# The order of TensorE's products in a planned kernel: products of one kind kept together, a larger reserve of buffers

## The chip, the cores and the metric

One core of one Trainium2 chip runs the kernel. The metric is the device time of one launch in microseconds (us); before the change it is 470.25 us, the median of 3 runs (469.52 to 470.39). The engines are TensorE (PE in the profile: matrix products; PEld: loading their weights), VectorE (DVE), ScalarE (ACT), GpSimd (POOL) and SyncE (SP), which issues DMA transfers.

## The reference

One layer of a hybrid decoder for a prompt of 1024 new tokens and 8 sequences of 8 sample tokens, 1088 tokens of 1024 features. All is float32. Cut to what matters:

```python
h = rms_norm(x, norm_g)
a, gl, zc, q, k, v, zg, lr = split(h @ w_in)            # 1024 x 3088
# group 1: a causal convolution
u  = a * sigmoid(gl)
cv = depthwise_causal_conv(u, conv_w, conv_b)           # 31 taps, 512 channels
cv = silu(group_layer_norm(cv, cn_g, cn_b))
cv = (cv @ w_pw + b_pw) * silu(zc)
# group 2: gated linear attention, 4 heads, keys 64, values 128
g  = log_sigmoid(lr @ w_alpha + b_alpha) / 16           # lr has rank 16
# per chunk of 64 tokens, B = cumsum(g):
o  = (q * exp(B)) @ S + mask((q * exp(B)) @ (k * exp(-B)).T) @ v
S  = S * exp(B_last) + (k * exp(B_last - B)).T @ v
o  = rms_norm_per_head(o) * gla_g * silu(zg)
y  = rms_norm(x + concat(cv, o) @ w_out, final_g)
```

Besides y the kernel writes the last 30 rows of u and the states S, for the prompt and for each sample.

## The kernel before

Features or channels lie on the 128 partitions, tokens along the free axis. The tokens are cut into chunks of 384, 384 and 320 (line 24), the last 64 of which are the sample tokens. The large products are made in three passes of the type f32r, each factor split into a high and a low part (hh and hl of the normed input, h_ and l_ of a weight); in the profile p_a, p_gl, p_q, p_k, p_zc and p_zg are such projections by chunk, and pv0_0 to pv0_8 and pv1_0 to pv1_8 the value projection by tiles of 128 tokens for the two pairs of heads (v_tile, line 645). Small products, transposes and the attention are plain f32: lrtp (a transpose), pk (transposed keys), px (keys times values), pa (scores), po (outputs, from the state S and from the masked scores at), pos, pas and pSs (samples).

The tile pv0_n also carries the 16 gate features. VectorE splits them into the buffers lrst0 and lrst1 in turn; TensorE transposes such a buffer (lrtp, lines 690 and 691), ScalarE copies it to lrT, and from three of these the gates of a chunk are made (gates, line 705: a product pg, then exp, ln, a cumulative sum B as a scan on VectorE, and the factors ge and g). Only then can q, k and the attention of that chunk follow (gla_states, line 765; gla_out, line 797). The heads are normed by o_norm (line 918): ScalarE squares o into osq, the square is split into on_h and on_l, TensorE sums each over the partitions (on_2p for the third chunk), and VectorE scales o.

The depthwise convolution runs on VectorE: for each of four tiles of channels 31 instructions over 1024 tokens (SCALAR_TENSOR_TENSOR cv<-u,par,cv; the first is a TENSOR_SCALAR), called taps here. For the samples ScalarE writes the 31 scaled rows into pr, and VectorE adds them up in two TENSOR_REDUCEs (conv_start, line 551).

The order of the instructions isn't written out by hand. Each instruction is recorded as an Op with a cost in ns (add, line 142; the costs stand at the helpers, lines 320 to 398) and a priority, which is its number in the program's order; taps get 1048576 more (conv_tick) and so fill whatever else leaves free. The planner (schedule, lines 183 to 290) then plays the program on a model of the engines: whenever an engine is free it takes from the instructions whose inputs are ready the one of the lowest priority whose buffers can be had. The buffers are slots of a few tags ("unit": 11 of 128x384); can_alloc (line 212) leaves free slots for tiles that come earlier in the program, at most as many as the tag's reserve says. In the order of the planned starts the instructions are issued (issue, line 292), each engine runs its own in that order, and the semaphores between them are set by the data. The plan's times thus set the order on every engine, and nothing else.

## Time and profile before

| | |
|---|---|
| device time, median of 3 runs | 470.25 us (469.52 to 470.39) |
| the profiled execution | 470.04 us |
| its span | 467.9 us |
| mean granted clock of TensorE | 0.995 of full |
| TensorE busy | 458.9 us (98%) |
| VectorE busy | 401.1 us (86%) |
| ScalarE busy | 304.4 us (65%) |
| TensorE busy from 36 to 450 us | 414.00 of 414.00 us |

The span runs from the first instruction to the last; the execution's time has some 2 us more around it. A busy share counts the time in which at least one instruction of the engine is under way. Instructions of one engine overlap at their ends: a tap lasts 1.28 us and the next one starts 1.20 us after it, and a product's record is longer than the distance to the next. What an instruction costs its engine is therefore the distance between starts, not its length. A granted clock of 1.00 is the upper of TensorE's two levels, 2.4 GHz.

### The profile page before, as it was taken

What the parts mean: (1) busy time and instruction counts of PE and PEld (TensorE: products, weight loads), DVE (VectorE), ACT (ScalarE), POOL (GpSimd) and SP (SyncE); (2) the same over time, 40 slices, a digit from 0 to 9 for tenths busy, and PEclk for the clock granted to TensorE, in tenths of its full rate; (3) what the DMA queues carried; (4) which work ended last, traced back from release to release, by engine and by line L of the source; (5) the groups of instructions that cost most, each with busy time, mean ns of one, the idle gap of its engine ahead of it and who ended that gap; (6) DMA issues with size and microseconds to landing.
All of it is one profiled execution on the core that took longest, in us unless ns stands there. A gap on an engine that the chain in (4) does not pass through costs nothing.

```text
span 467.9 us, 7864 instructions
## 1 busy us (share of the span) xinstructions
PE 458.9 (98%) x2867; PEld 431.2 (92%) x2867; DVE 401.1 (86%) x634; ACT 304.4 (65%) x780; POOL 19.3 (4%) x39
## 2 busy tenths in 40 slices
PE   8999999999999999999999999999999999999994
PEld 7899999999999999999999999999999988888783
DVE  4999998999999989999888999995548848988674
ACT  6978649926670545685634696544899548878636
POOL 1000000000000000000000000000000023130000
PEclk9999999999999999999999999999999999999998
DMA  8910283313012110022021011102235392386754
GB/s 253 352 57 1 93 205 57 54 51 69 1 59 78 36 56 6 35 73 77 20 71 39 14 47 45 46 22 73 88 78 181 87 228 48 68 182 154 242 174 179
DMA packets 33238, 43.28 MB, mean 92 GB/s; under 512 B 11696, under 2 KB 16560, under 8 KB 33200
## 3 DMA queue, kind: packets, MB, share of 16 engines
q1 hardware_dynamic: 30896, 38.59, 26.5%
q0 software_dynamic: 2304, 4.20, 5.5%
q8 instruction: 22, 0.36, 0.3%
q14 instruction: 16, 0.13, 0.1%
HBM read 36.58 MB, written 6.19 MB: 91 GB/s over the span
## 4 chain that ended last, share of the span: by engine, by line
PE 88%; DMA 4%; DVE 3%; ACT 3%; issue 1%; SPq 1%; DVEq 0%
PE pv L389 11%; PE p_zc L389 10%; PE p_zg L389 10%; PE p_gl L389 8%; PE p_a L389 8%; PE ya L389 7%; PE p_k L389 5%; PE p_q L389 5%; PE pw L389 5%; PE yc L389 5%; PE po L389 2%; PE pys L389 2%; DMA xr<-in_x 1%; DVE xr L343 1%; DMA s_gl<-in_w_in 1%; DMA s_a<-in_w_in 1%
## 5 line engine op out<-in xcount | busy, mean ns | idle before, releaser
L339 DVE SCALAR_TENSOR_TENSOR cv<-u,par,cv 128x1024 f32<-128x1024 f32 x120 | 150.8, 1278 | 0.2
L389 PE MATMUL pv<-h_v,hh 128*128 128x272 f32 (+1 forms) x128 | 37.4, 292 | 0.0
L389 PE MATMUL pv<-h_v,hl 128*128 128x272 f32 (+1 forms) x128 | 37.1, 290 | 0.0
L389 PE MATMUL pv<-l_v,hh 128*128 128x272 f32 (+1 forms) x128 | 36.8, 288 | 0.0
L333 ACT ACTIVATE pr<-us,par 128x64 f32<-128x64 f32 x124 | 32.3, 343 | 2.4 <-DMA us<-in_cc 2.4
L389 PE MATMUL p_gl<-hh,h_gl 128*128 128x384 f32 (+1 forms) x96 | 32.5, 339 | 0.8 <-ACT hh L333 0.8
L389 PE MATMUL p_zc<-hh,h_zc 128*128 128x384 f32 (+1 forms) x96 | 32.0, 333 | 0.0
L389 PE MATMUL p_gl<-hl,h_gl 128*128 128x384 f32 (+1 forms) x96 | 31.7, 330 | 0.2 <-DVE hl L343 0.2
L389 PE MATMUL p_a<-hh,l_a 128*128 128x384 f32 (+1 forms) x96 | 31.8, 331 | 0.0
L389 PE MATMUL p_a<-hh,h_a 128*128 128x384 f32 (+1 forms) x96 | 31.5, 328 | 0.1
L389 PE MATMUL p_zc<-hh,l_zc 128*128 128x384 f32 (+1 forms) x96 | 31.5, 329 | 0.0
L389 PE MATMUL p_zc<-hl,h_zc 128*128 128x384 f32 (+1 forms) x96 | 31.5, 328 | 0.0
L389 PE MATMUL p_gl<-hh,l_gl 128*128 128x384 f32 (+1 forms) x96 | 31.5, 328 | 0.0
L389 PE MATMUL p_zg<-hh,l_zg 128*128 128x384 f32 (+1 forms) x96 | 31.5, 328 | 0.0
L389 PE MATMUL p_zg<-hl,h_zg 128*128 128x384 f32 (+1 forms) x96 | 31.4, 327 | 0.0
L389 PE MATMUL p_zg<-hh,h_zg 128*128 128x384 f32 (+1 forms) x96 | 31.4, 327 | 0.0
L389 PE MATMUL p_a<-hl,h_a 128*128 128x384 f32 (+1 forms) x96 | 31.4, 327 | 0.0
L389 PEld LDWEIGHTS pv<-h_v,hh 128*128 128x128 f32 x128 | 24.1, 188 | 0.6 <-issue 0.2
L389 PEld LDWEIGHTS pv<-h_v,hl 128*128 128x128 f32 x128 | 24.1, 188 | 0.3 <-issue 0.3
L389 PEld LDWEIGHTS pv<-l_v,hh 128*128 128x128 f32 x128 | 24.1, 189 | 0.2
L389 PEld LDWEIGHTS p_gl<-hh,h_gl 128*128 128x128 f32 x96 | 18.1, 189 | 1.7 <-ACT hh L333 1.2
L389 PEld LDWEIGHTS p_gl<-hl,h_gl 128*128 128x128 f32 x96 | 18.2, 189 | 0.9 <-DVE hl L343 0.5
(337 smaller groups left out, 1306.8 us busy)
## 6 DMA issues: line engine op xcount, KB each, us to landing
xr<-in_x SPq DMA_DIRECT2D x16, 256.0 KB, 4.4
out_y<-xr SPq DMA_DIRECT2D x16, 256.0 KB, 2.3
x<-in_xT SPq DMA_DIRECT2D x16, 192.0 KB, 4.5
T<-in_w_out POOLq DMA_DIRECT2D x12, 256.0 KB, 5.1
s_gl<-in_w_in SPq DMA_DIRECT2D x8, 256.0 KB, 4.9
s_a<-in_w_in SPq DMA_DIRECT2D x8, 256.0 KB, 4.1
s_zc<-in_w_in SPq DMA_DIRECT2D x8, 256.0 KB, 2.6
s_zg<-in_w_in SPq DMA_DIRECT2D x8, 256.0 KB, 2.7
```

The lines of the kernel that those rows point to most:

```text
L333: return S.activation(R(out), R(in_), func, **kw)
L339: return prog.add("DVE", lambda: V.scalar_tensor_tensor(R(out), R(a), R(s), R(b), op0, op1), [out], [a, s, b], out.n / 0.96 + 67 + 62 * is ...
L343: return prog.add("DVE", lambda: V.tensor_tensor(R(out), R(a), R(b), op), [out], [a, b], out.n / 0.96 + 67)
L389: o = prog.add("PE", lambda: T.matmul(R(ps), R(lhsT), R(rhs), start=start, stop=stop, skip_group_check=True), [ps], [lhsT, rhs], c / 2 if ...
```

## The change

The planner's model of TensorE and its choice are changed in four places. (1) Each TensorE Op gets a kind, true for f32r products and false for plain f32 ones and transposes. When TensorE is free, the planner also looks for the ready Op of lowest priority among those of the kind that ran last; if its number is less than that of the best Op plus 60 (STICK), it is taken instead. For such a choice can_alloc is asked strictly, so that all earlier tiles' slots are left free. (2) A change of kind is charged 90 ns in the plan. (3) An f32r product is charged n/2.4 + 14 ns in place of n/2.4 + 2.5 for n columns. (4) The reserve of the tag "unit" is 8 in place of 6.

```diff
--- before.py
+++ after.py
@@ -47,6 +47,7 @@
 STATES_AT = 1
 CN_LAST = 2
 ADD_LAG = 5000
+STICK = 60
 SQ_SUM = (2, 4, 8)
 MARGIN = 20
 NWARM = 10
@@ -126,7 +127,7 @@
 
 class Op:
     __slots__ = ("eng", "fn", "cost", "lag", "table", "prio", "seq", "deps", "users", "wait", "ready", "tiles",
-                 "allocs", "start", "end", "bytes", "name")
+                 "allocs", "start", "end", "bytes", "name", "kind")
 
 
 class Program:
@@ -139,9 +140,10 @@
         self.last_pe = None
         self.chain = None
 
-    def add(self, eng, fn, outs, ins, cost, table=None, nbytes=0, lag=0):
+    def add(self, eng, fn, outs, ins, cost, table=None, nbytes=0, lag=0, kind=None):
         o = Op()
         o.eng, o.fn, o.cost, o.table, o.bytes, o.lag = eng, fn, cost, table, nbytes, lag
+        o.kind = kind
         o.seq = len(self.ops)
         o.prio = o.seq + (LOW if self.low else 0)
         if eng == "PE" and self.step:
@@ -208,15 +210,18 @@
         holder = {}
         dma = [0.0, 0.0]
         done = []
-
-        def can_alloc(o, t):
+        kind = [None]
+
+        def can_alloc(o, t, strict=False):
             need = {}
             for tl in o.tiles:
                 if tl.tag in free_at and tl.slot is None:
                     need.setdefault(tl.tag, []).append(tl.first)
             for tag, firsts in need.items():
                 have = sum(1 for f in free_at[tag] if f <= t)
-                before = min(bisect_left(pend[tag], min(firsts)), self.reserve.get(tag, 1 << 30))
+                before = bisect_left(pend[tag], min(firsts))
+                if not strict:
+                    before = min(before, self.reserve.get(tag, 1 << 30))
                 if have < len(firsts) + before:
                     return False
             return True
@@ -230,18 +235,24 @@
             t, e = heapq.heappop(events)
             if t < t_free[e]:
                 continue
-            best = None
+            best = same = None
             nxt = None
             for o in avail[e]:
                 if o.ready <= t:
                     if (best is None or o.prio < best.prio) and can_alloc(o, t):
                         best = o
+                    if (e == "PE" and o.kind == kind[0] and (same is None or o.prio < same.prio)
+                            and can_alloc(o, t, True)):
+                        same = o
                 elif nxt is None or o.ready < nxt:
                     nxt = o.ready
             if best is None:
                 if nxt is not None:
                     heapq.heappush(events, (nxt, e))
                 continue
+
+            if same is not None and same.prio < best.prio + STICK:
+                best = same
             o = best
             avail[e].remove(o)
             o.start = t
@@ -249,6 +260,9 @@
             if o.table is not None and table[0] != o.table:
                 table[0] = o.table
                 cost += 1300
+            if e == "PE" and o.kind != kind[0]:
+                kind[0] = o.kind
+                cost += 90
             if e == "SP":
                 t_free[e] = t + 60
                 dma[0] = max(dma[0], t) + 450
@@ -313,7 +327,7 @@
     ctx = ExitStack()
     V, S, G, T = nc.vector, nc.scalar, nc.gpsimd, nc.tensor
     prog = Program({"big": NBIG, "unit": NUNIT, "wst": NST, "wl": NW, "wh": NW, "ps": 8, "kT": 2, "S": 6, "ss": 9},
-                   {"ps": 3, "unit": 6, "big": 2})
+                   {"ps": 3, "unit": 8, "big": 2})
 
     TABLES = {AF.Exp: "natural_log_exp_and_others", AF.Ln: "natural_log_exp_and_others",
               AF.Sigmoid: "sigmoid_and_others", AF.Silu: "silu_and_others"}
@@ -385,9 +399,9 @@
     def mm(ps, lhsT, rhs, start, stop, after=(), pair=False):
         n, m = rhs.n, lhsT.n
         lag = 150 if m <= 64 and not R_DT(rhs) else 0
-        c = max(n / 2.4 + 2.5, m / 1.2) if R_DT(rhs) else max(n / 1.2 + 2.5, m / 1.2) + max(n / 1.2 if m > 64 else 53, m / 1.2)
+        c = max(n / 2.4 + 14, m / 1.2) if R_DT(rhs) else max(n / 1.2 + 2.5, m / 1.2) + max(n / 1.2 if m > 64 else 53, m / 1.2)
         o = prog.add("PE", lambda: T.matmul(R(ps), R(lhsT), R(rhs), start=start, stop=stop, skip_group_check=True),
-                     [ps], [lhsT, rhs], c / 2 if pair else c, lag=lag)
+                     [ps], [lhsT, rhs], c / 2 if pair else c, lag=lag, kind=R_DT(rhs))
         o.deps.update(a for a in after if a is not None)
         return o
 
@@ -395,7 +409,7 @@
         return v.tile.dt == F32R
 
     def transpose(out, in_, idn):
-        return prog.add("PE", lambda: T.transpose(R(out), R(in_), R(idn)), [out], [in_, idn], 109)
+        return prog.add("PE", lambda: T.transpose(R(out), R(in_), R(idn)), [out], [in_, idn], 109, kind=False)
 
     with ctx:
         fixed = ctx.enter_context(tc.tile_pool(name="fixed", bufs=1))
```

All engines have the same instructions as before, in another order. Lines of the kernel after are 14 higher where they lie behind line 212 or so (L389 becomes L403).

VectorE before the change, where the gates of tiles 5 to 7 are prepared (lrst1 and lrst0 are the split gate features, cv0 and cv1 taps of the first two channel tiles, g0_1 the gate of the second chunk):

```order
L339 SCALAR_TENSOR_TENSOR cv1_830<-u1_294,par_86,cv1_830 128x1024
L343 TENSOR_TENSOR gc0_1591<-gd0_1572,gm0_1552 128x2
L343 TENSOR_TENSOR lrst1_133<-pv0_5_1516,lrst1_133 128x16 x2
L339 SCALAR_TENSOR_TENSOR cv0_727<-u0_381,par_86,cv0_727 128x1024
L339 SCALAR_TENSOR_TENSOR cv1_830<-u1_294,par_86,cv1_830 128x1024
L349 TENSOR_SCALAR g0_1_1632<-pg0_1_1614,par_86 128x384
L343 TENSOR_TENSOR lrst0_127<-pv0_6_1565,lrst0_127 128x16 x2
L339 SCALAR_TENSOR_TENSOR cv1_830<-u1_294,par_86,cv1_830 128x1024
L343 TENSOR_TENSOR g0_1_1632<-g0_1_1632,ge0_1_1627 128x384
L343 TENSOR_TENSOR lrst1_133<-pv0_7_1610,lrst1_133 128x16 x2
```

VectorE after, from the same lrst1<-pv0_5 to the same lrst1<-pv0_7:

```order
L357 TENSOR_TENSOR lrst1_133<-pv0_5_1529,lrst1_133 128x16
L353 SCALAR_TENSOR_TENSOR cv1_826<-u1_291,par_86,cv1_826 128x1024
L357 TENSOR_TENSOR gc0_1620<-gd0_1600,gm0_1589 128x2
L357 TENSOR_TENSOR lrst1_133<-pv0_5_1529,lrst1_133 128x16
L353 SCALAR_TENSOR_TENSOR cv1_826<-u1_291,par_86,cv1_826 128x1024
L378 TENSOR_REDUCE pr2_1_1140<-pr2_0_1087 128x64
L357 TENSOR_TENSOR lrst0_127<-pv0_6_1575,lrst0_127 128x16 x2
L363 TENSOR_SCALAR g0_1_1661<-pg0_1_1653,par_86 128x384
L353 SCALAR_TENSOR_TENSOR cv1_826<-u1_291,par_86,cv1_826 128x1024
L363 TENSOR_SCALAR cv2_1682<-u2_944,par_86 128x1024
L357 TENSOR_TENSOR g0_1_1661<-g0_1_1661,ge0_1_1659 128x384
L357 TENSOR_TENSOR lrst1_133<-pv0_7_1630,lrst1_133 128x16 x2
```

Between the two there are now taps of cv1 in all gaps, the first tap of cv2 (the TENSOR_SCALAR of 1024) and a TENSOR_REDUCE of the samples; two more TENSOR_REDUCEs stand a few rows further up.

TensorE before, at the attention of the third chunk (po<-ge,S and pa are part-array products, pv1_1 and pv1_2 are f32r):

```order
L389 MATMUL pv1_1_2084<-l_v13_1743,hh7_248 128x256
L389 MATMUL pv1_1_2084<-h_v13_1719,hl7_262 128x256
L389 MATMUL po0_2_0_2127<-ge0_2_1889,S0_5_2033 128x128
L389 MATMUL po0_2_1_2129<-ge0_2_1889,S0_5_2033 128x128
L389 MATMUL pv1_2_2131<-h_v10_1667,hh0_147 128x256
L389 MATMUL pa0_2_0_2134<-ge0_2_1889,g0_2_1904 128x128
L389 MATMUL pa0_2_1_2136<-ge0_2_1889,g0_2_1904 128x128
L389 MATMUL pa0_2_0_2134<-ge0_2_1889,g0_2_1904 128x128
L389 MATMUL pa0_2_1_2136<-ge0_2_1889,g0_2_1904 128x128
L389 MATMUL po0_2_0_2127<-ge0_2_1889,S0_6_2122 128x128
L389 MATMUL po0_2_1_2129<-ge0_2_1889,S0_6_2122 128x128
L389 MATMUL pv1_2_2131<-l_v10_1682,hh0_147 128x256
```

TensorE after, the first of these po behind px of the same chunk:

```order
L403 MATMUL po0_1_1_2001<-at1_102,v0_0_1367 128x128
L403 MATMUL po0_1_1_2001<-at1_102,v0_4_1540 128x128 x2
L403 MATMUL px0_2_2118<-v0_4_1540,kT0_2_2104 64x128 x4
L403 MATMUL po0_2_0_2124<-ge0_2_1886,S0_5_2060 128x128
L403 MATMUL po0_2_1_2126<-ge0_2_1886,S0_5_2060 128x128
L403 MATMUL pv1_1_2100<-h_v10_1688,hh1_155 128x256
L403 MATMUL pv1_1_2100<-l_v10_1713,hh1_155 128x256
```

TensorE after, the pa of the same chunk:

```order
L403 MATMUL pv1_2_2157<-h_v13_1740,hl7_258 128x256
L403 MATMUL pa0_2_0_2188<-ge0_2_1886,g0_2_1918 128x128
L403 MATMUL pa0_2_1_2190<-ge0_2_1886,g0_2_1918 128x128
L403 MATMUL pa0_2_0_2188<-ge0_2_1886,g0_2_1918 128x128
L403 MATMUL pa0_2_1_2190<-ge0_2_1886,g0_2_1918 128x128
L403 MATMUL po0_2_0_2124<-ge0_2_1886,S0_6_2147 128x128
L403 MATMUL po0_2_1_2126<-ge0_2_1886,S0_6_2147 128x128
L412 MATMUL pxs0_2202<-cst_799,g0_2_1918 64x128
L403 MATMUL pas0_2204<-q20_2193,g0_2_1918 64x64 x2
L403 MATMUL pv1_3_2215<-h_v10_1688,hh0_147 128x256
```

The two po<-ge,S0_5 have moved up to px and share one run with it; pa, po<-ge,S0_6, pxs and pas now follow one another with no f32r product between.

## Rows read from the trace of the kernel before

**Rows 1.** The page, section 1: busy us, share of span, instructions.

```profile
PE 458.9 (98%) x2867; PEld 431.2 (92%) x2867; DVE 401.1 (86%) x634; ACT 304.4 (65%) x780; POOL 19.3 (4%) x39
```

**Rows 2.** By stage: busy us and instructions per engine, granted clock, DMA share, GB/s.

```profile
36.00:450.00 414.00, 414.00 (x2636) 391.39 (x2635) 360.93 (x553) 266.65 (x693) 17.24 (x26) 1.00 0.29 80
```

**Rows 3.** What TensorE waited for: us in total, times, longest.

```profile
PE p_gl L389 <- ACT hh L333: 0.8, 1, 0.8
PE p_gl L389 <- DVE hl L343: 0.2, 1, 0.2
```

**Rows 4.** The page, section 4: shares of the chain that ended last.

```profile
PE 88%; DMA 4%; DVE 3%; ACT 3%; issue 1%; SPq 1%; DVEq 0%
```

**Rows 5.** By stage, as Rows 2, in two stretches of the middle.

```profile
49.40:134.30 84.90, 84.90 (x562) 84.90 (x561) 81.17 (x105) 54.21 (x193) 0.12 (x1) 1.00 0.32 73
134.30:209.88 75.58, 75.58 (x591) 71.37 (x590) 72.37 (x108) 40.62 (x124) 1.44 (x4) 1.00 0.15 51
```

**Rows 6.** TensorE's timeline: start, length, instruction, tiles.

```profile
212.46 0.33 PE L389 MATMUL p_k<-hh,l_k 128*128 128x384 f32 x1
212.63 0.33 PE L389 MATMUL p_k<-hh,h_k 128*128 128x384 f32 x1
```

**Rows 7.** TensorE's timeline round a run of px.

```profile
149.64 0.34 PE L389 MATMUL p_k<-hh,l_k 128*128 128x384 f32 x1
149.91 0.88 PE L389 MATMUL px<-v,kT 128*64 128x128 f32 x12
151.17 0.35 PE L389 MATMUL p_k<-hh,l_k 128*128 128x384 f32 x1
```

**Rows 8.** TensorE by line and form: busy us, mean ns.

```profile
L389 PE MATMUL px<-v,kT 128*64 128x128 f32 x64 | 4.8, 282 | 0.0
L389 PE MATMUL po<-at,v 128*128 128x128 f32 x64 | 8.1, 275 | 0.0
```

**Rows 9.** TensorE's timeline round a run of po<-at.

```profile
157.04 0.31 PE L389 MATMUL p_q<-hh,h_q 128*128 128x320 f32 x1
157.19 1.50 PE L389 MATMUL po<-at,v 128*128 128x128 f32 x12
158.68 0.31 PE L389 MATMUL p_q<-hh,l_q 128*128 128x320 f32 x1
```

**Rows 10.** VectorE by line and form, 49.4 to 219 us: busy us, mean ns.

```profile
L339 DVE SCALAR_TENSOR_TENSOR cv<-u,par,cv 128x1024 f32<-128x1024 f32 x78 | 97.8, 1278 | 0.0
L364 DVE TENSOR_REDUCE pr<-pr 128x64 f32<-128x1024 f32 x4 | 7.9, 1974 | 1.4 <-ACT pr L333 1.4
L354 DVE TENSOR_TENSOR_SCAN B<-cst,g 128x384 f32<-128x384 f32 x4 | 3.8, 950 | 0.0
L349 DVE TENSOR_SCALAR cv<-u,par 128x1024 f32<-128x1024 f32 x4 | 3.2, 803 | 0.0
```

**Rows 11.** VectorE's timeline: seven taps in a row.

```profile
88.06 8.46 DVE L339 SCALAR_TENSOR_TENSOR cv<-u,par,cv 128x1024 f32<-128x1024 f32 x7
```

**Rows 12.** VectorE's timeline: lrst of tiles 4 and 7.

```profile
125.67 0.23 DVE L343 TENSOR_TENSOR lrst<-pv,lrst 128x16 fp32r<-128x16 f32 x2
134.15 0.26 DVE L343 TENSOR_TENSOR lrst<-pv,lrst 128x16 fp32r<-128x16 f32 x2
```

**Rows 13.** TensorE's timeline: the transpose of tile 7.

```profile
134.75 0.27 PE L398 MATMUL lrtp<-cst,lrst 128*128 128x128 f32 x1
```

**Rows 14.** TensorE's timeline at lrtp4's new place.

```profile
127.45 0.29 PE L389 MATMUL pv<-l_v,hh 128*128 128x272 f32 x1
127.58 0.29 PE L389 MATMUL pv<-h_v,hl 128*128 128x272 f32 x1
```

**Rows 15.** VectorE's timeline: on_2l of head 1, then o.

```profile
209.47 0.49 DVE L343 TENSOR_TENSOR on_2l<-osq,on_2h 128x320 fp32r<-128x320 f32 x1
209.88 0.61 DVE L339 SCALAR_TENSOR_TENSOR o<-o,par,osq 128x384 f32<-128x384 f32 x1
```

**Rows 16.** VectorE's longest wait, 47 to 140 us.

```profile
DVE pr L364 <- ACT pr L333: 1.4, 1, 1.4
```

## The prediction

> **What bounds the kernel now.** I read the page's busy shares first: TensorE 98%, VectorE 86%, ScalarE 65% [rows 1]. A share that high says that TensorE is the bound, not where it could cease to be, so the table by stages came next: from 36 to 450 us TensorE is busy for 414.00 of 414.00 us at a granted clock of 1.00 [rows 2]. The list of what TensorE waited for holds, once its products run, 0.8 and 0.2 us, both in the start [rows 3]. The chain that ended last gives it 88%, VectorE 3% [rows 4]. So a change of TensorE's order can win only what lies between products (the time lost where their kind changes), and it can lose whatever waits it brings in. For that I looked at who has slack against TensorE, engine by engine, in the stretch where the small attention products are. ScalarE works 54.21 of 84.90 us there and 40.62 of 75.58: far from full. VectorE works 81.17 of 84.90 and 72.37 of 75.58 [rows 5]. It has 3.73 + 3.21 = 6.94 us to spare before 209.88 us and no more. This is the number on which the prediction turns.
>
> **The change part by part.** No instruction is added or removed on any engine; all that changes is the order, through four edits to the planner: the preference for one kind of product, 90 ns charged for each change of kind, 11.5 ns more for each f32r product, and a reserve of 8 unit buffers in place of 6.
>
> *Products grouped by kind.* Planned runs of plain f32 products get fewer: 103 changes of kind become 63. The planner's price of 90 ns would make this 40 x 0.09 = 3.6 us. The rows say otherwise. Round the 12 px products, which use half of the array's columns (128*64), the starts run from 149.64 to 151.17, 1.53 us. In it are three f32r products of 384 columns at 0.174 (0.17 from start to start in [rows 6]) = 0.52, and 12 px at (0.88 - 0.28)/11 = 0.055 = 0.65, with 0.282 the mean length of one [rows 7, 8]. Left over: 0.36 us. Round the 12 po<-at products, f32 too but on the full array, 157.04 to 158.68 is 1.64 us; two products of 320 columns at 0.174 x 320/384 = 0.145 and 12 at (1.50 - 0.275)/11 = 0.111 make 1.62 [rows 8, 9]. Left over: 0.02. So what costs is not the precision but the part of the array, and about 0.36 us for each run of part-array products. There are 23 such runs now and 19 after, 13 and 10 before 213 us, 10 and 9 behind it. Four runs fewer are 4 x 0.36 = 1.4 us. Boundaries of px to po<-S inside a run, or of full to part f32, stand in no row: from 0 to the full 0.36 each, which leaves the saving between 0.4 and 3.6 us. I take 1.4 for all of it, and 0.7 for the part behind 213 us (one run is 0.36, up to 1.7 with 13 unshown boundaries of full and part f32 free; nearer the lower end).
>
> On this the Trainium skill, "TensorE: Matmul & The Clock Gate", Part 2, step-by-step, has a rule: a weight load is pulled ahead of a running product only where row groups don't conflict or where it goes to the background buffer; precision is not among its conditions. The two pieces of trace above agree with it (0.36 us with part of the array, 0.02 with the whole, both f32). By it the saving is near the 1.4; by the planner's own price it would be 3.6.
>
> *Right cost of f32r products: VectorE.* 384 columns were planned at 162.5 ns and are now planned at 174, which is what they take: 212.46 to 212.63 [rows 6]. That sounds harmless, but it is what moves VectorE's work. The conv taps (1024-wide SCALAR_TENSOR_TENSOR) have the lowest priority and fill each gap that the plan sees on VectorE. A plan in which TensorE is slower has longer gaps before each due piece of work, and so more taps ahead of it. Until now the plan was about 7% too fast on TensorE, and this hid that it is too fast on VectorE as well: it books a TENSOR_REDUCE at 1024/0.96 + 67 = 1134 ns, and it takes 1974; a scan at 467, and it takes 950 [rows 10]. With the first error mended and the second left, VectorE's queue is too long for the times it was made for, and in-order engines don't skip.
>
> First place: lrst1<-pv0_7, which the transpose lrtp of v tile 7 waits for. In the new order it has ahead of it, more than now and with nothing less, 4 taps x 1.197 (from the row of seven, (8.46 - 1.28)/6, so that neighbours overlap by 0.08), 3 reduces x (1.97 - 0.08) and a 1024-wide TENSOR_SCALAR at 0.80 - 0.08 = 0.72 [rows 10, 11]: 4.79 + 5.67 + 0.72 = 11.18 us. In the kernel before it ends at 134.15 + 0.26 = 134.41, and TensorE's transpose starts at 134.75 [rows 12, 13]; slack 0.3. The queue in front of it can give back at most the 3.73 us of idle time since 49.40 (up to there VectorE's orders are the same), or 4.9 if at each of some 15 waits the 0.08 of overlap is idle time too. So it ends at 134.41 + 11.18 - 4.9 = 140.7 or later. The transpose stands five products later in TensorE's order, 5 x 0.13 us (127.45 to 127.58): it could start at 135.4 [rows 14]. TensorE is 5.3 us late there, and all the products behind it stand still with it. The greatest single piece of that is at lrtp of tile 4, whose lrst0 has 5 taps and 2 reduces more and one scan less ahead of it, 5.99 + 3.78 - 0.87 = 8.9 us: it ends now at 125.67 + 0.23, so after at 130 to 130.5 at the earliest (4.4 to 4.9 of idle time won back), against 127.45 at its new place on TensorE, some 3 us [rows 10 to 12, 14].
>
> Second place: on1_2l, which TensorE's on1_2p products need (the l half of a split sum of squares). By here 14 taps and three pieces of the head norms o (two of 384 at 0.61 - 0.08 = 0.53, one of 320 at 0.46) have moved ahead of it: 14 x 1.197 + 1.52 = 18.28 us [rows 11, 15]. It ends now at 209.47 + 0.49 = 209.96. Idle before it is 6.94 us, 9.1 with the overlap at some 27 waits. After: 209.96 + 18.28 - 9.1 = 219.1 at the earliest, 221.3 if only the rows' 6.94 is won back. Its product moves from place 1305 to 1316 in TensorE's order, and the product now at place 1316 starts at 212.63 [rows 6]. TensorE is late by 219.2 - 212.63 = 6.6 us, 8.7 at the other end. These aren't added to the 5.3: it is the same queue, and the later floor holds the earlier in it. Behind it the two orders meet again: the taps that were brought forward are missing later, VectorE gains slack, and the last 623 products are the same. From place 1316 to the span's end TensorE has 467.9 - 212.63 = 255.3 us of work, and no slack in it to win the delay back [rows 2].
>
> *The reserve of unit buffers* only changes when a product or tap may be planned; its effect is in the counts above. ScalarE's and GpSimd's orders: ScalarE has 30 us free in each stretch [rows 5], which hides a shift of a few us; if it didn't, VectorE's waits on ScalarE would return (1.4 us is the longest now, [rows 16]), and I put 0.5 us for these, from 0 to 1.4. The start moves two products and no wait that I can see: 0, within 0.3 either way, by the waits there now [rows 3]. SP's queue keeps its order but for a few neighbours; 0, since TensorE waits for no DMA now, up to 0.8, as long as the longest wait in the start, if it did [rows 3].
>
> **Sum.** The profiled execution took 470.04 us, of which the span is 467.9; the median of the runs is 470.25, so it is an ordinary one. 470.04 + 6.6 (second place, earliest) + 0.5 (VectorE's waits that remain) - 0.7 (switches saved behind it) = 476.4 us. Low end of this case: 6.6 with 1.7 saved and 0.3 won at the start, 474.6; high end 8.7 + 0.5 with 0.4 saved, 478.8.
>
> **Rivals.**
> - *Only the switches count (the other side).* TensorE's due times have enough room, because VectorE's idle time is larger than the profile shows, and the gain of 1.4 us stands: 468.6, between 466 and 469. For it: TensorE has no wait on VectorE in the whole middle now. Against it: it would have to find 18.28 us in a queue with 9.1. It decides as soon as the VectorE floor at on1_2l is under 212.6. Chance 0.06.
> - *Half absorbed.* The taps run faster than 1.197, or their inputs let VectorE start earlier: at 1.0 us each the floor falls by 14 x 0.2 = 2.8, and the idle time in the start adds 1 or 2: 469.2 to 473. Against it: the row of seven is without a wait. Chance 0.05, of which 0.03 within the band of no change.
> - *The clock falls.* The granted clock is 1.00 in all stages to 450 us, with waits of 0.8 us at most once the products run [rows 2, 3]. A wait of 3 us is in no row. If the clock fell to 1.2 GHz there, the 64 products from lrtp of tile 4 to that of tile 7 (some 8 us) would take up to 8 us more, of which part falls into the wait for tile 7 and about 3 to 6 us stay: 479 to 482. Chance 0.08. The Trainium skill, same page, Part 1 on the HAM clock gate, says that an idle TensorE is granted half of its clock; no run here shows it in the middle of a kernel, and by it this rival would be likelier than I make it.
> - *The forecast*, 474 to 479: 0.81.
>
> **Numbers.** Under 0.2% (0.9 us) this kernel's runs can't be told apart (469.52 to 470.39). Faster by more: the first rival, 0.06. Same: 0.03. Slower: 0.81 + 0.08 + 0.02 = 0.91. The range 473.2 to 479.8 holds the forecast's case to both its ends, a little of the absorbed one, and the milder part of the clock's; about 0.15 is left out.
>
> **What will show it.** Right: VectorE's share in the chain rises well above 3%; TensorE waits for lrst at several lrtp between 110 and 141 us, the longest near 3 us at tile 4; lrtp of tile 7 starts at 140.5 or later; on1_2p's l products wait and start behind 219 us; TensorE's stretch from 36 to 450 us has some 6 to 8 us of idle time, none of it behind about 285 us; the conv taps are done earlier. Part-array runs still cost about 0.36 us each, full-array ones nothing. Wrong: no TensorE wait on VectorE between 110 and 220 us, or lrtp of tile 7 before 140 us; then VectorE's durations or idle time were misread. If the waits are there and the time is still under 473 us, the switches gave more than I read from the rows.

## The result, and the profile after

The changed kernel takes 484.19 us (median of 4 runs, 481.88 to 485.24), the kernel before 469.88 in the same comparison: a ratio of 1.030, 95% interval 1.026 to 1.035. It is slower, as forecast, but by 14.3 us instead of 6.4, and outside the range of 473.2 to 479.8. The profiled execution took 484.95 us, span 483.1.

The page's busy shares and the chain that ended last, which answer to [rows 1, 4]:

```profile
PE 464.1 (96%) x2867; PEld 434.1 (90%) x2867; DVE 399.6 (83%) x634; ACT 303.0 (63%) x780; POOL 19.2 (4%) x39
...
PE 59%; DVE 17%; ACT 10%; DMA 7%; issue 4%; SPq 2%; DVEq 0%; ACTq 0%
...
```

TensorE's share of the chain fell from 88 to 59%; VectorE's rose from 3 to 17%, ScalarE's from 3 to 10%. What TensorE waited for behind the start (in total, times, longest; nothing like it in [rows 3]):

```profile
PE lrtp L412 <- DVE lrst L357: 3.1, 3, 1.6
PE pg L403 <- ACT lrT L347: 2.3, 2, 1.6
...
PE po L403 <- DVE at L375: 0.8, 1, 0.8
...
PE on_1p L403 <- DVE on_1l L357: 0.4, 1, 0.4
...
```

The table by stages, columns as in [rows 2]:

```profile
36.00:108.00 72.00, 72.00 (x424) 71.56 (x424) 69.74 (x89) 47.73 (x153) 0.25 (x2) 1.00 0.33 77
108.00:145.00 37.00, 31.29 (x236) 30.02 (x235) 36.94 (x57) 24.22 (x92) 0.00 (x0) 1.00 0.10 19
145.00:192.00 47.00, 46.15 (x363) 43.16 (x361) 46.97 (x65) 16.68 (x53) 0.62 (x2) 1.00 0.17 58
192.00:200.00 8.00, 8.00 (x45) 7.61 (x45) 6.06 (x10) 0.93 (x4) 0.41 (x1) 0.57 0.01 2
200.00:450.00 250.00, 249.64 (x1525) 233.25 (x1524) 190.22 (x324) 168.17 (x375) 15.92 (x21) 1.00 0.29 79
```

Read PE's busy time and PEclk. Between 108 and 145 us, while the gates are prepared, TensorE is idle for 37.00 - 31.29 = 5.71 us; VectorE is busy for 36.94 of these 37.00. Between 192 and 200 us TensorE is busy all the time at a granted clock of 0.57, a mean over the two levels. The last product starts 10.0 us ahead of the span's end, where it started 7.3 us ahead before.

The same products can be followed through both traces, at places of TensorE's order ahead of which both kernels have done the same work. The pv product at place 600 starts at 108.96 and 109.62 us: 0.7 us late, from the start. (The start differs from execution to execution: at this place the five profiled executions that have the changed kernel's order up to it are at 108.5 to 111.0 us, three with the order of before at 108.3 to 109.0; how much of the 0.7 is the new order's isn't shown.) At lrtp of tile 7 TensorE is 7.6 us late (143.01, against the 135.4 at which its new place came due). The p_zg product at place 1863 starts at 304.75 and 316.87: 12.1 us. The last product starts at 460.66 and 473.16: 12.5 us. The span ends 15.2 us later. So there are three large losses: about 7 us at the gates, 4.5 between there and 304 us, nearly all of it by 215 us, and 2.7 behind the last product.

**The gates.** VectorE's timeline round lrst of tile 4 and tile 7 [rows 12], and TensorE's at pg, lrtp of tile 4 and lrtp of tile 7 [rows 13]:

```profile
129.22 1.99 DVE L378 TENSOR_REDUCE cv<-pr 128x64 f32<-128x1024 f32 x1
131.14 1.27 DVE L353 SCALAR_TENSOR_TENSOR cv<-u,par,cv 128x1024 f32<-128x1024 f32 x1
132.34 0.54 DVE L357 TENSOR_TENSOR g<-g,ge 128x384 f32<-128x384 f32 x1
132.81 0.24 DVE L357 TENSOR_TENSOR lrst<-pv,lrst 128x16 fp32r<-128x16 f32 x2
...
137.71 1.92 DVE L378 TENSOR_REDUCE pr<-pr 128x64 f32<-128x1024 f32 x1
...
142.63 0.24 DVE L357 TENSOR_TENSOR lrst<-pv,lrst 128x16 fp32r<-128x16 f32 x2
```

```profile
125.97 0.44 PE L403 MATMUL pg<-lrT,was 128*128 128x384 f32 x1 [1.59 <-ACT lrT L347]
...
133.19 0.30 PE L412 MATMUL lrtp<-cst,lrst 128*128 128x128 f32 x1 [1.26 <-DVE lrst L357]
...
143.01 0.30 PE L412 MATMUL lrtp<-cst,lrst 128*128 128x128 f32 x1 [0.25 <-ACT h_v L347]
```

(The last lrtp's wait is put down to ScalarE's h_v; its lrst had ended 0.14 us earlier, at 142.87.) TENSOR_REDUCEs and taps stand ahead of lrst now, of which the fence shows some; it ends at 142.87 for tile 7 where it ended at 134.41. TensorE's products behind a late lrtp wait too, and the gate product pg, whose lrT ScalarE can only copy after that lrtp, waits another 1.59 us. VectorE's idle time in the stretches that answer to [rows 5]:

```profile
49.40:142.63 93.23, 87.77 (x573) 86.61 (x571) 90.99 (x110) 58.12 (x208) 0.12 (x1) 1.00 0.29 66
142.63:223.97 81.34, 79.89 (x594) 75.32 (x593) 78.54 (x116) 37.14 (x110) 1.44 (x4) 0.96 0.16 53
```

93.23 - 90.99 = 2.24 and 81.34 - 78.54 = 2.80 us: of the 6.94 us of idle time before, 1.9 were won back.

**The clock.** TensorE's timeline where it changes level:

```profile
187.75 0.45 PE L403 MATMUL pas<-q,g 128*64 128x64 f32 x4
188.13 0.38 PE L403 MATMUL pv<-h_v,hh 128*128 128x256 f32 x1
189.36 1.16 PE L403 MATMUL po<-at,v 128*128 128x128 f32 x8 [0.85 <-DVE at L375]
190.35 0.56 PE L403 MATMUL pos<-ats,vs 128*128 128x64 f32 x4
190.75 2.38 PE L403 MATMUL pos<-q,S 128*128 128x16 f32 x16
192.96 0.56 PE L403 MATMUL pv<-l_v,hh 128*128 128x256 f32 x1
193.32 0.42 PE L403 MATMUL pv<-h_v,hl 128*128 128x256 f32 x1
193.54 0.41 PE L403 MATMUL pv<-h_v,hh 128*128 128x256 f32 x1
193.75 0.41 PE L403 MATMUL pv<-l_v,hh 128*128 128x256 f32 x1
```

TensorE waits 0.85 us for at, with small products on both sides of the wait (and one pv product directly ahead of it); then products of 256 columns, 0.12 us apart ahead of it, are 0.21 apart (193.54 to 193.75), the 1.2 GHz level. The granted clock is at that level from 192.0 to 198.8 us, 6.8 us.

**The end.** VectorE's last additions (TENSOR_TENSOR) and scalings (SCALAR_TENSOR_TENSOR), first of the changed kernel, then of the kernel before:

```profile
471.47 0.75 DVE L353 SCALAR_TENSOR_TENSOR xr<-xr,ss,fg 128x512 f32<-128x512 f32 x1 [1.35 <-ACT ss L347]
472.14 0.68 DVE L357 TENSOR_TENSOR xr<-ya,xr 128x512 f32<-128x512 f32 x1
474.18 0.75 DVE L353 SCALAR_TENSOR_TENSOR xr<-xr,ss,fg 128x512 f32<-128x512 f32 x1 [1.35 <-ACT ss L347]
474.85 1.28 DVE L357 TENSOR_TENSOR xr<-ya,xr 128x512 f32<-128x512 f32 x2
476.88 0.75 DVE L353 SCALAR_TENSOR_TENSOR xr<-xr,ss,fg 128x512 f32<-128x512 f32 x1 [0.76 <-ACT ss L347]
478.81 0.75 DVE L353 SCALAR_TENSOR_TENSOR xr<-xr,ss,fg 128x512 f32<-128x512 f32 x1 [1.18 <-ACT ss L347]
```

```profile
458.94 0.75 DVE L339 SCALAR_TENSOR_TENSOR xr<-xr,ss,fg 128x512 f32<-128x512 f32 x1 [1.18 <-ACT ss L333]
459.61 0.68 DVE L343 TENSOR_TENSOR xr<-ya,xr 128x512 f32<-128x512 f32 x1
461.09 0.69 DVE L343 TENSOR_TENSOR xr<-ya,xr 128x512 f32<-128x512 f32 x1 [0.79 <-PE ya L389]
461.70 0.74 DVE L339 SCALAR_TENSOR_TENSOR xr<-xr,ss,fg 128x512 f32<-128x512 f32 x1
463.58 0.75 DVE L339 SCALAR_TENSOR_TENSOR xr<-xr,ss,fg 128x512 f32<-128x512 f32 x1 [1.14 <-ACT ss L333]
```

Before, the last addition starts as soon as its product is there (461.09, after 0.79 us of waiting for PE). After, one addition stands behind a scaling that waits 1.35 us for ScalarE's ss (471.47), and the last two stand behind the next scaling, which waits 1.35 us again (474.18). Their blocks' squares, roots and scalings begin that much later: before, the last addition starts 0.4 us after the start of the last product, now 2.3 us after it. The last product starts 9.99 us ahead of the span's end; before it was 7.26.

### The profile page after: what moved, and what is told of

Its sections match the earlier page's. It is cut to its first block, busy times and chain, and to the rows that moved or that the text cites. A ratio compares the mean times of both kernels' runs of the same rounds, so it can differ in the third digit from the quotient of the medians.

```text
span 483.1 us, 7867 instructions
## 1 busy us (share of the span) xinstructions
PE 464.1 (96%) x2867; PEld 434.1 (90%) x2867; DVE 399.6 (83%) x634; ACT 303.0 (63%) x780; POOL 19.2 (4%) x39
## 4 chain that ended last, share of the span: by engine, by line
PE 59%; DVE 17%; ACT 10%; DMA 7%; issue 4%; SPq 2%; DVEq 0%; ACTq 0%
PE p_zc L403 10%; PE p_zg L403 10%; DVE cv L353 9%; PE p_k L403 5%; PE p_q L403 5%; PE pw L403 5%; PE ya L403 4%; PE pv L403 4%; PE p_gl L403 3%; PE p_a L403 3%; PE po L403 2%; SPq L391 2%; DMA xr<-in_x 2%; ACT sq L347 1%; DVE xr L357 1%
## 5 line engine op out<-in xcount | busy, mean ns | idle before, releaser
L403 PE MATMUL pv<-h_v,hl 128*128 128x272 f32 (+1 forms) x128 | 38.0, 297 | 0.0
L403 PE MATMUL pv<-h_v,hh 128*128 128x272 f32 (+1 forms) x128 | 37.8, 296 | 0.0
L403 PE MATMUL pv<-l_v,hh 128*128 128x272 f32 (+1 forms) x128 | 37.7, 294 | 0.0
L403 PE MATMUL p_gl<-hh,h_gl 128*128 128x384 f32 (+1 forms) x96 | 32.3, 336 | 1.1 <-ACT hh L347 0.6
L403 PE MATMUL p_gl<-hh,l_gl 128*128 128x384 f32 (+1 forms) x96 | 31.8, 331 | 0.2 <-DVE l_gl L357 0.2
L403 PE MATMUL p_gl<-hl,h_gl 128*128 128x384 f32 (+1 forms) x96 | 31.8, 332 | 0.1
L403 PE MATMUL p_a<-hh,l_a 128*128 128x384 f32 (+1 forms) x96 | 31.7, 330 | 0.0
L403 PE MATMUL p_zc<-hh,h_zc 128*128 128x384 f32 (+1 forms) x96 | 31.7, 330 | 0.0
L403 PE MATMUL p_a<-hh,h_a 128*128 128x384 f32 (+1 forms) x96 | 31.5, 328 | 0.2 <-ACT h_a L347 0.2
L403 PE MATMUL p_zc<-hh,l_zc 128*128 128x384 f32 (+1 forms) x96 | 31.6, 329 | 0.0
L403 PE MATMUL p_zc<-hl,h_zc 128*128 128x384 f32 (+1 forms) x96 | 31.5, 328 | 0.0
L403 PE MATMUL p_zg<-hh,l_zg 128*128 128x384 f32 (+1 forms) x96 | 31.4, 327 | 0.0
L403 PE MATMUL p_zg<-hl,h_zg 128*128 128x384 f32 (+1 forms) x96 | 31.4, 327 | 0.0
L403 PE MATMUL p_zg<-hh,h_zg 128*128 128x384 f32 (+1 forms) x96 | 31.4, 327 | 0.0
L403 PE MATMUL p_a<-hl,h_a 128*128 128x384 f32 (+1 forms) x96 | 31.4, 327 | 0.0
L403 PEld LDWEIGHTS pv<-h_v,hh 128*128 128x128 f32 x128 | 25.2, 197 | 0.4 <-issue 0.2
L403 PEld LDWEIGHTS pv<-h_v,hl 128*128 128x128 f32 x128 | 25.3, 197 | 0.2 <-issue 0.2
L403 PEld LDWEIGHTS pv<-l_v,hh 128*128 128x128 f32 x128 | 25.3, 198 | 0.0
L357 DVE TENSOR_TENSOR o<-o,zg 128x384 f32<-128x384 f32 (+1 forms) x12 | 6.2, 532 | 16.6 <-ACT zg L347 16.6
L403 PEld LDWEIGHTS p_gl<-hh,h_gl 128*128 128x128 f32 x96 | 18.0, 188 | 2.1 <-ACT hh L347 1.1
## 6 DMA issues: line engine op xcount, KB each, us to landing
x<-in_xT SPq DMA_DIRECT2D x16, 192.0 KB, 4.6
```

The source lines that it names most:

```text
L357: return prog.add("DVE", lambda: V.tensor_tensor(R(out), R(a), R(b), op), [out], [a, b], out.n / 0.96 + 67)
L403: o = prog.add("PE", lambda: T.matmul(R(ps), R(lhsT), R(rhs), start=start, stop=stop, skip_group_check=True), [ps], [lhsT, rhs], c / 2 if ...
```

## The experiments

Two theories stood against each other. A: the mended f32r cost alone makes VectorE's queue too long for TensorE. B: bringing the small products together costs time, through waits in a row and the clock. All comparisons are with runs of the kernel before on the same chip (469.9 to 470.0 us).

**The cost edit alone.**

```diff
-        c = max(n / 2.4 + 2.5, m / 1.2) if R_DT(rhs) else ...
+        c = max(n / 2.4 + 14, m / 1.2) if R_DT(rhs) else ...
```

> The kernel before with one of the four edits: an f32r product is planned at n/2.4 + 14 ns; no preference for a kind, no charge for a change, reserve 6. Theory A (the mended cost alone lengthens VectorE's queue): in this order 10.0 us more of VectorE's work than before stand ahead of lrst1<-pv0_7 (11.2 with all four edits) and 13.4 ahead of on1_2l (18.3), and the last adds of VectorE stand behind a scaling that waits for ScalarE, as in the changed kernel: TensorE waits 5 to 8 us for lrst and the gates, the span's end behind the last product grows by 2.7 us, 478 to 482 us, clock without a fall since pos stands between f32r products. Rival B (it is the grouping that costs: the small f32 products, brought together, wait in a row and let the clock fall): 470 to 473, the 2.7 us of the end at most.

481.30 us, ratio 1.0245 (1.021 to 1.028): A. One edit of the four brings 11.4 of the 14.3 us (with the longer end and the fall of the clock, below, in it). The waits are at lrtp:

```profile
PE lrtp L398 <- issue: 3.7, 1, 3.7
PE lrtp L398 <- DVE lrst L343: 1.4, 2, 0.7
```

The longest stands as "issue", but VectorE's lrst ends at 116.62, 0.09 us ahead of that lrtp, and VectorE is busy for 3.74 of 3.80 us in the stage shown next: it is VectorE's queue here too. But the clock did fall, against the expectation; the stages round that wait:

```profile
112.80:116.60 3.80, 0.23 (x2) 0.00 (x1) 3.74 (x8) 0.64 (x3) 0.00 (x0) 1.00 0.80 139
116.60:120.20 3.60, 3.49 (x19) 3.52 (x20) 3.60 (x6) 1.54 (x7) 0.00 (x0) 0.66 0.17 38
```

After this wait of 3.7 us and 1 us of products the granted clock goes to half, from 117.7 to 121.2 us, and the products between 117.7 and 120.5 us are 0.23 apart in place of 0.126. This is the rival that the prediction placed at lrtp.

**The other three edits alone.**

```diff
-        c = max(n / 2.4 + 14, m / 1.2) if R_DT(rhs) else ...
+        c = max(n / 2.4 + 2.5, m / 1.2) if R_DT(rhs) else ...
```

(to the changed kernel)

> The changed kernel without the mended f32r cost (n/2.4 + 2.5 as before); preference, charge and the reserve of 8 stay. TensorE's order has 17 part-array runs (23 before, 19 changed) and the same run of pa, po, pxs, pas, po, pos at the same place 1103 as the changed kernel; VectorE has only 1.2 us more ahead of lrst1<-pv0_7 and 3.5 ahead of on1_2l than before. Theory A: no slower than before, 468 to 471; 6 runs fewer at 0.36 us would make it 2 us faster if no wait takes that back. Rival B: the grouping costs, 476 to 485. On the clock: if the run of small products by itself lets it fall, the granted clock is 0.5 for some 5 us behind pos here too and the time 3 us longer; if it takes the wait of 0.85 us for at as well, the clock stays at 1.00.

469.86 us, ratio 0.9996 (0.998 to 1.002): no change. B falls as the cause of the 14 us. The run of small products stands at the same place as in the changed kernel and the granted clock of the profiled execution stays at 1.00 there. That the clock fell in none of the other executions isn't shown: four of the ten have a mean clock of 0.992 and took 469.8 to 470.7 us, five have 0.995 or 0.996 and took 467.7 to 470.0. The gain for six runs is in the trace (2.3 us, below), and so is a wait that takes most of it:

```profile
155.85 0.55 PE L412 MATMUL pk<-cst,g 128*128 128x128 f32 x3 [2.01 <-DVE g L357]
```

The transpose pk waits 2.01 us for VectorE's g, a wait that the kernel before didn't have: the transposes of the second chunk's keys have been drawn forward by 35 products, right behind the px of the first chunk, to follow other plain products.

**The end by itself.** Twice: in the changed kernel the products of 512 columns are planned as before; in the kernel before only these are planned at the new cost.

```diff
-        c = max(n / 2.4 + 14, m / 1.2)
+        c = max(n / 2.4 + (2.5 if n == 512 else 14), m / 1.2)
```

> The changed kernel, except that products of 512 columns (those of the output projection) are planned at n/2.4 + 2.5 as before; all orders up to the output products are those of the changed kernel. VectorE's last adds stand where they stood before. Theory: the end behind the last product is a term of its own, 2.7 us: 481.4 beside 484.2 of the changed kernel. Rival: the end is longer because the output transfers come late and close together; then this does nothing, 484.

482.73 us, only 1.5 less in the median, but the profiled execution (480.56) has its last product start 7.16 us ahead of the end, 2.8 less. It also differs by the clock: this execution, with the same order on TensorE throughout, has no fall, though it has the same wait for at. Its stages and the wait:

```profile
108.00:145.00 37.00, 31.96 (x241) 30.69 (x240) 36.94 (x55) 24.20 (x90) 0.00 (x0) 1.00 0.09 19
192.00:200.00 8.00, 8.00 (x74) 7.56 (x73) 8.00 (x14) 2.41 (x8) 0.41 (x1) 1.00 0.01 2
```

```profile
190.00 1.16 PE L403 MATMUL po<-at,v 128*128 128x128 f32 x8 [0.84 <-DVE at L375]
```

From the product at 186.14 us to the one at 205.22 it takes 19.08 us; the same products of the changed kernel start at 185.49 and 207.58, 22.09 us. The fall cost 3.0 us. The three other executions of this kernel had mean clocks of 0.987 to 0.991, against 0.998, and took 1.9 to 2.6 us more; two of the four of the changed kernel (0.987 and 0.988) took 485 us, the other two (0.993 and 0.994) 481.9 and 483.4. So the same order on TensorE has the fall in some executions and not in others. What decides it is not shown: in the two that were traced the wait is 0.85 and 0.84 us.

```diff
-        c = max(n / 2.4 + 2.5, m / 1.2)
+        c = max(n / 2.4 + (14 if n == 512 else 2.5), m / 1.2)
```

(to the kernel before)

> The kernel before, with the mended cost for products of 512 columns only (n/2.4 + 14; all others n/2.4 + 2.5). All orders up to the output products are those of before; VectorE's last adds and scalings have the order of the changed kernel, in which two adds of a block stand behind a scaling that waits for ScalarE. Theory: the end behind the last product goes from 7.3 to 10 us, 472.7 in all (2.7 more than 470.0). Rival: the end of the changed kernel is long for another reason (its transfers or a lower clock there), and this is within 0.3 us of before.

473.05 us, ratio 1.0073 (1.005 to 1.010): 3.1 us more, 10.19 us behind the start of the last product. TensorE's order is that of before to the last product, and VectorE's last rows have the waits of the changed kernel again (1.35, 1.35, 0.76 and 1.18 us for ss). So the longer end comes from the order on the other engines. Besides VectorE's, that of some ScalarE instructions and of a few loads of x differs too, and the runs don't separate these.

**VectorE's load taken away, the order kept.**

```diff
-  V.scalar_tensor_tensor(cv[:, :1024], u[:, j:j + 1024], w, cv[:, :1024], ...)
+  V.scalar_tensor_tensor(cv[:, :512], u[:, j:j + 512], w, cv[:, :512], ...)   # planned and ordered as 1024
```

> The changed kernel with every instruction in its place and order; each conv tap but the first of a channel tile computes only the first 512 of its 1024 columns (the convolution is left out for the other tokens), so that VectorE has some 0.53 us less per tap. Theory A (TensorE is late because VectorE's queue is too full in this order): the waits for lrst, the gates, at and on_l go, some 8 us, and with them the fall of the clock; left are the end's 2.7 us less the 4 part-array runs saved at 0.36: 469.5 to 473. Rival B (the order on TensorE itself makes the waits: transposes stand too close behind their products): still 478 to 485.

474.16 us, ratio 1.0084 (1.007 to 1.010); 10.0 us of the 14.3 are gone. TensorE's stages:

```profile
108.00:145.00 37.00, 36.02 (x267) 35.48 (x266) 30.79 (x64) 26.71 (x101) 0.00 (x0) 1.00 0.22 60
145.00:192.00 47.00, 47.00 (x395) 44.20 (x394) 35.36 (x65) 16.69 (x50) 1.04 (x3) 1.00 0.09 30
192.00:200.00 8.00, 8.00 (x68) 7.64 (x67) 5.83 (x12) 6.54 (x17) 0.41 (x1) 1.00 0.12 41
```

In 108 to 145 us it is idle for 0.98 in place of 5.71 us, all but the whole of it one wait of 1.0 us for lrT; the 0.85 us wait for at is gone and the clock stays at 1.00 though the run of small products is where it was. What remains is mainly 2.9 us at the end (10.19 us behind the last product) and that one wait. The expected range ended at 473: the wait for lrT was not in it.

> The kernel before with the same half taps, same order otherwise; the control for after_half. TensorE has no wait to lose there: 469 to 471, the same as before. If it were more than 1 us faster, VectorE would hold TensorE up before the change as well, by something that the list of waits doesn't show.

469.66 us, ratio 0.9995 (0.998 to 1.001): the control. VectorE costs the kernel before nothing that can be measured.

**The true costs on VectorE.**

```diff
 scan:  -  out.n / 0.96 + 67    +  out.n / 0.48 + 67
 vsum:  -  a.n / 0.96 + 67      +  a.n / 0.56 + 67
```

> The changed kernel with VectorE's two wrong costs mended as well: a TENSOR_REDUCE planned at 1.90 us instead of 1.13, a scan of 384 at 0.87 instead of 0.47. VectorE has 8.1 us more than before ahead of lrst1<-pv0_7 (11.2 in the changed kernel) and 8.3 ahead of on1_2l (18.3); the end's order is that of the changed kernel. Theory A: TensorE loses some 3 us at lrst in place of 7, nothing more behind, and 2.7 us at the end: 474 to 478. Rival (the two costs don't matter, the taps alone are too many): 482 to 485.

478.63 us, ratio 1.019 (1.016 to 1.023): 5.6 us better than the changed kernel, and above the expected range by 0.6. TensorE waits for lrst twice, 3.1 us in all and 2.3 at the longest, as expected; not expected was a fall of the clock behind the longer wait (122 to 125 us). So the two undercharged instructions are a part of it only. The end is the changed kernel's (10.4 us behind the last product), and TensorE still waits 3.1 us; that this is because the plan fills VectorE's gaps with taps and leaves nothing over is a reading, which the next run tries.

**Slack planned back in.** The last run keeps all four edits, has the true costs of VectorE, the old cost for 512 columns, and plans each tap at 1.08 of its cost.

```diff
-  stt(cv, u, w, cv)            # 1024 / 0.96 + 67 + 62
+  stt(cv, u, w, cv)            # (1024 / 0.96 + 67 + 62) * 1.08
```

> The changed kernel with all four edits, but with slack planned back in on VectorE: TENSOR_REDUCE and scan at what they take, each tap at 1.08 of its cost, and products of 512 columns at n/2.4 + 2.5 (VectorE's last adds stand as before the change). VectorE has 1.9 us more than before ahead of lrst1<-pv0_7 (11.2 in the changed kernel) and nothing more ahead of on1_2l (18.3); 17 part-array runs (23 before). Theory A (the mended f32r cost is harmless as long as the filler work leaves VectorE room): TensorE's waits of 8 us, the fall of the clock and the 2.7 us of the end are gone, some of the 6 x 0.36 = 2.2 us of saved runs is left: 467.8 to 470.5. Rival (a right cost for f32r products costs by itself, by an order of TensorE that can't be kept): 474 or more.

468.55 us, ratio 0.9978 (0.996 to 0.999). The waits for the gates are gone, but for 0.2 us at lrtp:

```profile
108.00:145.00 37.00, 36.82 (x271) 36.28 (x270) 36.59 (x62) 24.28 (x93) 0.00 (x0) 1.00 0.22 62
145.00:192.00 47.00, 47.00 (x399) 44.16 (x398) 45.16 (x66) 19.08 (x59) 1.45 (x4) 1.00 0.09 29
```

With the mended cost in place for all products but those of the output, the kernel is 0.2% faster than before. The end is 7.36 us. Three things were changed at once here, so the run shows that the mended cost can be kept, not how much each of the three gives.

**A better version.** The preference by part of the array:

```diff
-  kind=R_DT(rhs)
+  kind=R_DT(rhs) or (m > 64 and lhsT.part[1] - lhsT.part[0] > 64)     # transposes: True; f32r cost as before
-                cost += 90
+                cost += 180
```

> A version meant to be better: as no_cost, but the kind is not the precision but whether a product uses part of the array, and a change is charged 180 ns. 15 part-array runs (23 before, 17 in no_cost); VectorE has as much ahead of lrst1<-pv0_7 as before, 1.2 us more ahead of on1_2l. By the price of a run, 8 x 0.36 = 2.9 us less: 467.0 if no wait comes in. Rival: a wait for VectorE takes it back, as the 2.0 us at pk did in no_cost: 469 to 470.

468.82 us, ratio 0.9966 (0.995 to 0.998): 1.2 us of the 2.9. Fewer runs can account for it (2.3 us less between products, below), but no run separates them from the other shifts of order.

> geo180 with a margin of 60 ns instead of 20 in the planned latency of TensorE, VectorE and ScalarE, so that fewer instructions are planned to start just when their input lands, and with 120 in place of 60 for the preference. 14 part-array runs: 9 x 0.36 = 3.2 us less; VectorE has the same ahead of lrst1<-pv0_7 as before, 1.7 us more ahead of on1_2l. 466.5 to 468 without new waits; the order of VectorE's last adds is neither that of before nor that of the changed kernel, and could cost up to 2.7 us: 469 to 470 then.

467.21 us, ratio 0.9941 (0.992 to 0.996): the best, together with best2.

> The kernel before with a margin of 60 ns in place of 20 in the planned latencies and nothing else: is it the margin that made geo_margin 1.6 us faster than geo180, or what it does to the runs? 22 part-array runs (23 before): by their price 0.4 us less, by the end's order as in geo_margin (7.9 us behind the last product, 7.3 before) 0.6 more: 469.8 to 470.3. If the margin itself takes away small waits: 468 to 469.

467.72 us, ratio 0.9954 (0.994 to 0.997), against the expected 469.8 to 470.3: the margin of 60 ns in place of 20 does most of it by itself, 2.2 of 2.7 us. It isn't in the start: at place 189 of TensorE's order, 39.6 us here, before_half and before_512new, which have the order of before there, are at 39.8 and 39.7. At place 1194 it is 193.5 us against 194.9 and 194.7. Where these 1.2 to 1.3 us come from was not traced further.

> geo_margin with products of 512 columns planned at n/2.4 + 5, by which the order of VectorE's last seven adds and scalings is that of before: 7.3 us behind the last product in place of 7.9. 14 part-array runs as in geo_margin: 466.6. Rival: the end's order does nothing, 467.2.

467.17 us, ratio 0.9941 (0.992 to 0.996). The end is 0.4 us shorter (7.47 us behind the last product, 7.87), which the medians don't show.

## Why the prediction was wrong

- *What bounds.* Right. Before, TensorE had no slack and needed nothing of VectorE; halving VectorE's taps there changes nothing (before_half).
- *The price of a run.* About right: 0.36 us was read from one run of px. Full-array f32 costs nothing, as forecast. Counted from the product ahead of a run to the second product behind it, beyond the usual distances between starts, a run of px costs 0.34 us, most runs of pa and po 0.40 to 0.50, pSs 0.33 to 0.58. In sum that is 9.2 us before, 7.6 in after_half (19 runs, the changed kernel's order), 6.9 in no_cost without the wait at pk (17) and 6.9 in geo180 (15): 1.6 for four runs, 2.3 for six, 2.3 for eight. The boundaries that no row showed are neither free nor full: behind a run full-array f32 costs 0.05 us less than f32r, and px with po<-S in one run costs 0.54 where two runs cost 0.74. So joining two kinds of part-array products saves 0.20, not 0.36, which is why eight runs bring no more than six. In the changed kernel the saving is covered by the waits, in no_cost mostly by one.
- *The queue on VectorE.* The mechanism was right and its cause too: cost_only and after_half show that the mended cost and VectorE's load make the waits. lrst of tile 7 ended at 142.87, at or behind the 140.7 that was given, and lrtp started at 143.01. The size was off at one step: "at most the 3.73 us of idle time [...] or 4.9" was taken as wholly won back, and 9.1 at the second place (whose 219.2 is 219.1 by its own terms). At lrst of tile 7 only 134.41 + 11.18 - 142.87 = 2.7 us were given back, and of the 6.94 us of idle time up to the second place 1.9. TensorE was therefore 7.6 us late at the first place (6.9 without the start), not 5.3. The longest single wait was 1.6 us, for lrst of tile 1, not 3 at tile 4: TensorE came to tile 4 late already. The second place, on which the sum stood, decided nothing: on1_2l [rows 15] ended at 224.45, but its product, at 224.77, has no wait. TensorE came to it late already, by the gates, by 1.1 us more at at and 0.5 at on_1p, and by the clock. Counted between starts, and over 0.25 us, the waits come to 8.3 us: 6.7 at the gates (117 to 143 us) and those two.
- *The clock.* A rival with a chance of 0.08, priced at 3 to 6 us. It came in the profiled execution, 3.0 us, and by the mean clocks in about half of those of the changed kernel. It came at another place than was said, behind a wait of 0.85 us for at; at lrtp, where the prediction put it, it came in cost_only (a wait of 3.7 us) and in after_ve (2.3).
- *The end: the step that failed.* "The last 623 products are the same" was right (622 by the orders), and from it the prediction added nothing behind the last product. Only TensorE's order was looked at: the mended cost holds for the output's 512 columns too, and moved the last instructions of the other engines. It measured 2.7 us in the profile, 3.1 in before_512new.
- *The sum.* Waits less savings: 6.4 forecast, 8.8 measured (12.5 late at the last product, less 3.0 of clock and 0.7 in the start). That is the high end of the forecast's own case (8.7 + 0.5 - 0.4) and alone would have given 470.04 + 8.8 = 478.8 us, inside the range. With the end's 2.7 us it is 481.5 and outside, as were the two executions with the higher mean clocks (481.9 and 483.4); the clock's 3.0 and the start's 0.7 make up the 15.2 us of the span. Of the 8.8, the waits of over 0.25 us are 8.3 and the savings 1.6; the remaining 2.1 are shorter distances that weren't traced one by one.

## What to carry to other kernels

A planner's wrong cost can be what keeps the plan feasible. Here the bottleneck engine was planned too fast, the others got slack that nobody had asked for, and mending that one number without leaving room on the engine that fills its gaps moved the bound there (481.3 us with this edit alone, 468.6 with slack planned back in). When a cost changes, compare the order of every engine to its end, the bottleneck's neighbours above all, and don't count another engine's idle time as available until what ends each wait is known. A short wait can cost more through the clock than by its length: here one of 0.85 us among small products was followed by a fall that cost 3.0 us, in one of two traced executions.

## What was not expected of the hardware

- In the changed kernel's profiled execution the granted clock fell to the 1.2 GHz level for 6.8 us, behind a TensorE wait of 0.85 us in which nearly only small products were near (16 to 128 columns). With the same order and a wait of 0.84 us, after_512old's had no fall. It fell as well behind a wait of 3.7 us in cost_only and one of 2.3 us in after_ve; behind one of 2.0 us at pk in no_cost it did not.
- Changing between parts of the array costs time on both sides (medians over the traces, distances between starts beyond the usual): into a part from the full array 0.09 us, and 0.05 (128*64) or 0.10 (64*128) more between its first products; out of it 0.20 us to f32r and 0.15 to full-array f32, over the next two products; between the two shapes of part 0.10 us, and the 0.05 or 0.10 again.
